# The loads of the modulation weights, issued from POOL's queue instead of SP's

## The chip, the cores and the metric

The kernel runs on one core of a Trainium2 chip. The metric is device time in microseconds (us), the median of several runs. A profiled execution gives the trace; its span runs from the first instruction to the last.

The core has five engines with an instruction queue each: PE (matmul; its weight loads are listed as PEld), DVE, ACT, POOL (all three elementwise) and SP, which here only issues transfers. Each queue is worked through in order.

## The reference, cut to what matters

A decoder trunk of two layers on one sequence of 512 tokens, 1024 wide. Every sub-layer sees its input normalised, scaled and shifted by a modulation that comes from one conditioning vector `c`, and its output is multiplied by a gate from the same modulation:

```
cond = silu(c)
for layer in range(2):
    mod = cond @ ada_w[layer] + ada_b[layer]        # ada_w[layer]: 1024 x 6144
    shift_m, scale_m, gate_m, shift_f, scale_f, gate_f = split(mod, 6)
    h = rms_norm(x) * (1 + scale_m) + shift_m
    mixed = mixer(h) @ w_out                        # layer 0: S5 and HGRN2; layer 1: GLA
    x = x + gate_m * mixed
    h = rms_norm(x) * (1 + scale_f) + shift_f
    x = x + gate_f * ((silu(h @ w1) * (h @ w3)) @ w2)
return rms_norm(x)
```

All values are float32. `ada_w` has 12 pieces of 1024 x 1024 floats: six for each layer.

## The kernel before

**Activations and products.** Tokens lie along the free dimension: a tile is 128 features x 512 tokens. A matmul in full precision is made of three: `proj` (L269) splits each weight tile and each activation into a high and a low part and sums high x high, high x low and low x high. For each weight tile `wload` (L253) loads `raw` from SP (`wraw`, L241, three buffers), ACT copies it to `whi` and DVE subtracts to get `wlo` (`wsplit`, L246, three buffers each). So PE lives on splits that ACT and DVE make some tiles ahead.

**Modulation.** Two pieces, shift and scale of layer 0's mixer, are computed at once at the start (`ada_first`, L390) from loads of their own (L383). The other ten are made step by step beside the products. `ada_run` (L192) is a generator: for each entry of `later` it runs 8n steps on DVE, n = 4 for two pieces together, n = 2 for one. A step multiplies 128 x 512 weights by a column of `cond` and adds them to `acc` (L204, the first of an entry is L202); at the end four small matmuls fold `acc` over the partitions (L210). The steps keep their program order on DVE.

**Their loads.** `ada_loads` (L179) feeds the steps. One tile `wr` (tag "ar", two buffers) is 128 x 2 x 512 floats, 512 KB, and serves two steps. It is filled by n transfers: four of 32 partitions (128 KB) or two of 64 partitions (256 KB). In program order the tile for the next pair of steps is asked for one pair ahead. There are 64 tiles of four transfers and 16 of two, 288 in all. The first tiles also wait for `bn` and `cn`, S5 inputs that use the same two buffers (L649).

**Where the steps fall.** `ada_steps` (L226) is called at the end of each `wload` and runs up to `pace[0]` steps, up to a number of pieces. In layer 0's mixer the pace is 3 and later 8, in the FFN 2 for each weight tile. `ada_need` (L233) runs what is left when a piece is used: the gate of the mixer's output (L431), the norm ahead of the FFN (L366), the FFN's gate. In `later` the order is: layer 0's pieces 2 and 4, then 3, then 5, then three pairs for layer 1, which are made during layer 0's FFN.

**What sets the order.** The tile framework plans the order of each engine's instructions with a timing model (`schedule_with_timeline_sim`, L1252), and it places every wait. A transfer waits for its buffer to be free, on the engine that issues it, and what is queued behind it waits as well.

**POOL's own work.** In layer 0's mixer POOL makes the S5 matrices (`cmul` in `s5_mats`, L698: tiles `B0a`, `W0a` and so on), parts of the S5 rotation (`rz0c`, `rz0d` and their like, L788 to L800, between DVE's scans of L792), and gates (`hg`, `ys`). Later it has only sums for the norms (`na_f`, `na_m`, L335) and the gates of layer 1 (`gr`). It issues no transfer.

Of the kernel before, what the change touches and what calls it, by code (L numbers as in the profile page):

```python
# [19 lines left out]
T = 512  # L20
# [21 lines left out]
def trunk(  # L42
# [8 lines left out]
    nc = tc.nc  # L51
    x = x[0]
    out = out[0]
# [125 lines left out]
    def ada_loads():  # L179
        for l, pieces in later:  # L180
            n = 2 * len(pieces)
            r = P // n
            src = ada_w[l].rearrange("(k z r) n -> k r z n", z=2, r=r)
            for k in range(4 * n):
                wr = wp.tile([P, 2, T], F32, tag="ar", name=f"ar{l}{pieces[0]}{k}", bufs=2)
                for g in range(n):
                    c0 = pieces[g // 2] * D + g % 2 * T
                    nc.sync.dma_start(out=wr[g * r : g * r + r], in_=src[k, :, :, c0 : c0 + T])
                for j in range(2):
                    yield wr[:, j, :]  # L190

    def ada_run():  # L192
        loads = ada_loads()
        nxt = [next(loads) for _ in range(2)]
        for l, pieces in later:
            n = 2 * len(pieces)
            acc = ap.tile([P, T], F32, tag="acc", name=f"acc{l}{pieces[0]}", bufs=1)
            for k in range(8 * n):
                nxt.append(next(loads, None))
                w, c_ = nxt.pop(0), conds[n][:, k : k + 1]  # L200
                if k == 0:
                    ins = V.tensor_scalar(out=acc, in0=w, scalar1=c_, scalar2=None, op0=ALU.mult)  # L202
                else:
                    ins = V.scalar_tensor_tensor(out=acc, in0=w, scalar=c_, in1=acc, op0=ALU.mult, op1=ALU.add)  # L204
                tc.keep_in_program_order(ins)
                if k + 1 < 8 * n:
                    yield
            fp = ps_b(f"fold{l}{pieces[0]}")[:, 0 : 4 * n]
            for m in range(4):
                ins = PE.matmul(fp[:, m::4], lhsT=acc[:, m * P : (m + 1) * P], rhs=ind[n], start=True, stop=True)  # L210
                if m == 0:
                    tc.keep_in_program_order(ins)
            for j, i in enumerate(pieces):
                c0 = i * 8
                ttv(V, mod[:, l, c0 : c0 + 8], fp[:, j * 8 : j * 8 + 8], cols1[:, l * 48 + c0 : l * 48 + c0 + 8], ALU.add)
                if i in (1, 4):
                    g0 = 96 + (i // 4) * 16 + l * 8
                    stt(gsc[:, l * 2 + i // 4, :], mod[:, l, c0 : c0 + 8], 1.0, cols1[:, g0 : g0 + 8], ALU.add, ALU.mult)
                done.add((l, i))
            yield  # L220
# [921 lines left out]
    for hd in range(4):  # L1142
# [18 lines left out]
        c0 = 1024 + hd * 256  # L1161
        vt = tok_tiles(win[:, c0 : c0 + 2 * P], f"gv{hd}", keep, tag)
        c0 = 2048 + hd * 256
# [92 lines left out]
```

## Time and profile before

| | |
|---|---|
| median of 3 runs | 1357.15 us |
| lowest and highest | 1355.7, 1358.05 us |
| profiled execution | 1364.62 us |
| its span | 1362.8 us |
| its mean granted clock of PE | 0.967 of full |

The profiled execution lies 7.47 us above the median and its span 1.82 us below its own time. Times in the views count from the start of the span.

### The profile page before, as it was taken

What the parts mean: (1) busy time and instruction counts of PE and PEld (TensorE: products, weight loads), DVE (VectorE), ACT (ScalarE), POOL (GpSimd) and SP (SyncE); (2) the same over time, 40 slices, a digit from 0 to 9 for tenths busy, and PEclk for the clock granted to TensorE, in tenths of its full rate; (3) what the DMA queues carried; (4) which work ended last, traced back from release to release, by engine and by line L of the source; (5) the groups of instructions that cost most, each with busy time, mean ns of one, the idle gap of its engine ahead of it and who ended that gap; (6) DMA issues with size and microseconds to landing.
All of it is one profiled execution on the core that took longest, in us unless ns stands there. A gap on an engine that the chain in (4) does not pass through costs nothing.

```text
span 1362.8 us, 18262 instructions
## 1 busy us (share of the span) xinstructions
PE 1286.2 (94%) x6949; PEld 1103.4 (81%) x6949; DVE 797.2 (58%) x1511; ACT 487.5 (36%) x851; POOL 151.0 (11%) x148
## 2 busy tenths in 40 slices
PE   6598899799899999999999999999899999999997
PEld 3377887778888888888889999998788888888886
DVE  4979796887865566665445446557653333333344
ACT  5253556423532322222334434432442322232232
POOL 1764451120100000000000000000100000000000
PEclk9779998889899999999999999999999999999999
DMA  8624540534067768987333232213223323433222
GB/s 293 163 63 129 150 140 16 126 94 132 18 142 188 202 174 213 214 219 198 106 106 94 65 92 63 74 49 97 62 82 104 93 74 103 117 93 93 79 86 83
DMA packets 222824, 159.69 MB, mean 117 GB/s; under 512 B 16752, under 2 KB 195248, under 8 KB 222736
## 3 DMA queue, kind: packets, MB, share of 16 engines
q1 hardware_dynamic: 221696, 157.48, 42.2%
q10 hardware_dynamic: 1040, 1.05, 0.3%
q8 instruction: 54, 0.88, 0.3%
q14 instruction: 34, 0.28, 0.1%
HBM read 156.40 MB, written 2.10 MB: 116 GB/s over the span
## 4 chain that ended last, share of the span: by engine, by line
PE 78%; DVE 12%; DMA 4%; ACT 2%; issue 2%; POOL 1%; SPq 0%; DVEq 0%; ACTq 0%
PE f L275 18%; PE f L276 18%; PE f L277 18%; DMA ar<-in_ada_w_dram 3%; PE op L276 2%; PE op L275 2%; PE op L277 2%; PE lv_g L465 2%; DVE acc L204 2%; PE gr L300 1%; PE gr L301 1%; PE gr L299 1%; PE gv L301 1%; PE gv L300 1%; PE gv L299 1%
## 5 line engine op out<-in xcount | busy, mean ns | idle before, releaser
L276 PE MATMUL f<-hlo_f,whi_f 128*128 128x512 f32 (+1 forms) x736 | 281.5, 383 | 0.2 <-DVE hlo_f L116 0.2
L275 PE MATMUL f<-hhi_f,whi_f 128*128 128x512 f32 (+1 forms) x736 | 280.9, 384 | 0.5 <-ACT hhi_f L86 0.5
L277 PE MATMUL f<-hhi_f,wlo_f 128*128 128x512 f32 (+1 forms) x736 | 280.8, 382 | 0.0
L86 ACT ACTIVATE whi_f<-raw_f 128x1024 fp32r<-128x1024 f32 x88 | 93.3, 1061 | 307.0 <-PE f L276 169.3
L107 DVE TENSOR_TENSOR wlo_f<-raw_f,whi_f 128x1024 fp32r<-128x1024 f32 x88 | 107.7, 1224 | 115.1 <-ACT whi_f L86 114.8
L276 PEld LDWEIGHTS f<-hlo_f,whi_f 128*128 128x128 f32 x736 | 140.1, 190 | 27.0 <-DVE hlo_f L116 0.8
L275 PEld LDWEIGHTS f<-hhi_f,whi_f 128*128 128x128 f32 x736 | 139.8, 191 | 27.0 <-ACT hhi_f L86 1.0
L277 PEld LDWEIGHTS f<-hhi_f,wlo_f 128*128 128x128 f32 x736 | 140.1, 191 | 26.5
L204 DVE SCALAR_TENSOR_TENSOR acc<-ar,cond,acc 128x512 f32<-128x512 f32 x154 | 120.1, 780 | 41.6 <-DMA ar<-in_ada_w_dram 40.0
L277 PE MATMUL f<-hi_g,wlo_c 128*128 128x512 f32 x312 | 121.7, 390 | 0.0
L276 PE MATMUL f<-lo_g,whi_c 128*128 128x512 f32 x312 | 121.6, 390 | 0.0
L275 PE MATMUL f<-hi_g,whi_c 128*128 128x512 f32 x312 | 121.2, 390 | 0.0
L86 ACT ACTIVATE whi_c<-raw_c 128x768 fp32r<-128x768 f32 (+1 forms) x56 | 44.9, 801 | 161.8 <-PE f L276 114.1
L107 DVE TENSOR_TENSOR g<-g,f 128x512 f32<-128x512 f32 x44 | 30.3, 688 | 109.3 <-PE f L277 109.3
L107 DVE TENSOR_TENSOR wlo_c<-raw_c,whi_c 128x768 fp32r<-128x768 f32 (+1 forms) x56 | 50.3, 898 | 57.6 <-ACT whi_c L86 57.5
L276 PEld LDWEIGHTS f<-lo_g,whi_c 128*128 128x128 f32 x312 | 58.6, 188 | 12.1
L275 PEld LDWEIGHTS f<-hi_g,whi_c 128*128 128x128 f32 x312 | 58.6, 188 | 12.1
L277 PEld LDWEIGHTS f<-hi_g,wlo_c 128*128 128x128 f32 x312 | 58.6, 188 | 12.1
L116 DVE SCALAR_TENSOR_TENSOR x<-f,mod,x 128x512 f32<-128x512 f32 (+1 forms) x36 | 24.8, 689 | 39.4 <-PE f L277 39.2
L107 POOL TENSOR_TENSOR na_m<-na_m,nsq_m 128x256 f32<-128x256 f32 x7 | 5.7, 818 | 365.3 <-DMA raw_c<-in_ffn_w_dram 337.9
L300 PE MATMUL gv<-wlo_gv,hhi_m 128*128 128x256 f32 x128 | 36.7, 287 | 0.0
L301 PE MATMUL gv<-whi_gv,hlo_m 128*128 128x256 f32 x128 | 36.6, 286 | 0.0
(667 smaller groups left out, 2677.9 us busy)
## 6 DMA issues: line engine op xcount, KB each, us to landing
raw_f<-in_ffn_w_dram SPq DMA_DIRECT2D x88, 512.0 KB, 3.8
ar<-in_ada_w_dram SPq DMA_DIRECT2D x256, 128.0 KB, 3.7
ar<-in_ada_w_dram SPq DMA_DIRECT2D x64, 256.0 KB, 5.3
raw_c<-in_ffn_w_dram SPq DMA_DIRECT2D x32, 384.0 KB, 3.5
raw_c<-in_ffn_w_dram SPq DMA_DIRECT2D x24, 320.0 KB, 3.2
raw_gv<-in_od_w_in_dram SPq DMA_DIRECT2D x8, 512.0 KB, 4.4
raw_gr<-in_od_w_in_dram SPq DMA_DIRECT2D x8, 512.0 KB, 4.0
raw_o<-in_ev_w_out_dram SPq DMA_DIRECT2D x8, 384.0 KB, 3.4
```

The lines of the kernel that those rows point to most:

```text
L86: return A.activation(out=o, in_=i, func=f, **kw)
L107: e.tensor_tensor(out=o, in0=a, in1=b, op=op)
L116: V.scalar_tensor_tensor(out=o, in0=a, scalar=s, in1=b, op0=op0, op1=op1)
L204: ins = V.scalar_tensor_tensor(out=acc, in0=w, scalar=c_, in1=acc, op0=ALU.mult, op1=ALU.add)
L275: PE.matmul(ps, lhsT=hi, rhs=ah[:, ts], start=(i == 0), stop=False)
L276: PE.matmul(ps, lhsT=hi, rhs=al[:, ts], start=False, stop=False)
L277: ins = PE.matmul(ps, lhsT=lo, rhs=ah[:, ts], start=False, stop=(i == n - 1))
L299: PE.matmul(o, lhsT=ah[:, s], rhs=hi, start=(k == 0), stop=False)
L300: PE.matmul(o, lhsT=ah[:, s], rhs=lo, start=False, stop=False)
L301: PE.matmul(o, lhsT=al[:, s], rhs=hi, start=False, stop=(k == KT - 1))
L465: PE.matmul(ps[0:nk, w, :].rearrange("p (n b) -> p n b", b=b), lhsT=K[:, w * P : w * P + nk], rhs=qv[:, w * nb : (w + 1) * nb, b:], start= ...
```

## The change

Only the queue on which the loads of `ada_loads` are issued is another: POOL's (`nc.gpsimd`) for SP's (`nc.sync`). The tiles, their buffers, the 288 transfers, their sizes and the steps that use them stay. The loads of L383 stay on SP.

```
@@ -185,7 +185,7 @@
                 wr = wp.tile([P, 2, T], F32, tag="ar", name=f"ar{l}{pieces[0]}{k}", bufs=2)
                 for g in range(n):
                     c0 = pieces[g // 2] * D + g % 2 * T
-                    nc.sync.dma_start(out=wr[g * r : g * r + r], in_=src[k, :, :, c0 : c0 + T])
+                    nc.gpsimd.dma_start(out=wr[g * r : g * r + r], in_=src[k, :, :, c0 : c0 + T])
                 for j in range(2):
                     yield wr[:, j, :]
```

## Rows read from the trace of the kernel before

**Rows 1.** The page's totals: busy us, share of the span, instructions.

```profile
PE 1286.2 (94%) x6949; PEld 1103.4 (81%) x6949; DVE 797.2 (58%) x1511; ACT 487.5 (36%) x851; POOL 151.0 (11%) x148
```

**Rows 2.** The chain that ended last, share by engine and by line.

```profile
PE 78%; DVE 12%; DMA 4%; ACT 2%; issue 2%; POOL 1%; SPq 0%; DVEq 0%; ACTq 0%
PE f L275 18%; PE f L276 18%; PE f L277 18%; DMA ar<-in_ada_w_dram 3%; PE op L276 2%; PE op L275 2%; PE op L277 2%; PE lv_g L465 2%; DVE acc L204 2%; PE gr L300 1%; PE gr L301 1%; PE gr L299 1%; PE gv L301 1%; PE gv L300 1%; PE gv L299 1%
```

**Rows 3.** Busy time by stretch: length, engines, clock, DMA share, GB/s.

```profile
95.00:153.00 58.00, 50.48 (x306) 45.32 (x306) 48.64 (x95) 28.14 (x62) 24.06 (x16) 0.94 0.52 145
153.00:195.00 42.00, 37.15 (x301) 36.37 (x299) 40.42 (x70) 18.76 (x43) 17.98 (x15) 0.96 0.52 139
250.00:285.00 35.00, 27.48 (x139) 24.78 (x139) 29.23 (x76) 17.96 (x47) 5.32 (x4) 0.80 0.57 135
...
495.00:565.00 70.00, 70.00 (x314) 58.09 (x313) 42.62 (x59) 14.89 (x18) 0.00 (x0) 1.00 0.85 203
```

**Rows 4.** Line L188 over the whole span: ns min/median/max; who waited for it.

```profile
L188 SPq DMA_DIRECT2D ar<-in_ada_w_dram x288: 311/421/1852, 63.4 to 657.2; - x144
  DVE acc L204: 40.0, 25
```

**Rows 5.** Waits by engine (us, times, longest), 60 to 375, then 375 to 700.

```profile
DVE acc L204 <- DMA ar<-in_ada_w_dram: 10.6, 5, 4.2
SPq L188 <- DVE acc L204: 26.5, 14, 5.9
...
DVE acc L204 <- DMA ar<-in_ada_w_dram: 29.4, 20, 3.1
SPq L188 <- DVE acc L204: 70.1, 52, 3.8
```

**Rows 6.** The page's DMA queues: packets, MB, share of 16 engines.

```profile
q1 hardware_dynamic: 221696, 157.48, 42.2%
q10 hardware_dynamic: 1040, 1.05, 0.3%
```

**Rows 7.** POOL in order of time: start, us, instruction, idle time before it.

```profile
115.31 7.25 POOL L107 TENSOR_TENSOR rz0c<-rz0c,rz0d 128x512 f32<-128x512 f32 x1 [24.73 <-DVE rz0d L107]
126.28 1.26 POOL L107 TENSOR_TENSOR rz0d<-rz0d,cos 128x512 f32<-128x512 f32 x1
142.40 0.74 POOL L107 TENSOR_TENSOR B2b<-B2b 128x256 f32<-128x256 f32 x1
157.57 3.27 POOL L107 TENSOR_TENSOR rz1c<-rz1c,rz1d 128x512 f32<-128x512 f32 x1 [12.54 <-DVE rz1d L107]
193.88 5.41 POOL L107 TENSOR_TENSOR rz2c<-rz2c,rz2d 128x512 f32<-128x512 f32 x1 [7.48 <-DVE rz2d L107]
```

**Rows 8.** Line L188 from 95 to 153, 153 to 195, 250 to 285 us.

```profile
L188 SPq DMA_DIRECT2D ar<-in_ada_w_dram x36: 311/425/672, 101.6 to 148.8; - x36
  DVE acc L204: 5.2, 2
...
L188 SPq DMA_DIRECT2D ar<-in_ada_w_dram x24: 311/424/710, 153.1 to 191.4; - x24
...
L188 SPq DMA_DIRECT2D ar<-in_ada_w_dram x16: 595/597/608, 254.5 to 283.4; - x16
```

**Rows 9.** DVE in order of time in the FFN: steps on `acc`.

```profile
523.44 1.54 DVE L204 SCALAR_TENSOR_TENSOR acc<-ar,cond,acc 128x512 f32<-128x512 f32 x2 [1.00 <-DMA ar<-in_ada_w_dram]
...
531.67 1.54 DVE L204 SCALAR_TENSOR_TENSOR acc<-ar,cond,acc 128x512 f32<-128x512 f32 x2 [0.93 <-DMA ar<-in_ada_w_dram]
...
563.17 1.54 DVE L204 SCALAR_TENSOR_TENSOR acc<-ar,cond,acc 128x512 f32<-128x512 f32 x2 [2.81 <-DMA ar<-in_ada_w_dram]
```

**Rows 10.** SP's queue in order of time in the FFN.

```profile
525.01 1.72 SPq L188 DMA_DIRECT2D ar<-in_ada_w_dram  x4
526.83 0.39 SPq L243 DMA_DIRECT2D raw_c<-in_ffn_w_dram  x1
```

**Rows 11.** Line L188 from 495 to 565 us, and its transfers' time to landing.

```profile
L188 SPq DMA_DIRECT2D ar<-in_ada_w_dram x61: 311/418/1208, 496.3 to 564.7; - x61
...
DMA to landing us min/median/max: 2.5/5.3/6.9
```

More of the change, by code (lines that the diff above doesn't have):

```diff
@@ L187, in ada_loads @@
                     c0 = pieces[g // 2] * D + g % 2 * T
-                    nc.sync.dma_start(out=wr[g * r : g * r + r], in_=src[k, :, :, c0 : c0 + T])
+                    nc.gpsimd.dma_start(out=wr[g * r : g * r + r], in_=src[k, :, :, c0 : c0 + T])
                 for j in range(2):
```

## Prediction

> **What bounds the kernel now.** I read the page's totals first, then the chain that ended last, then busy time by stretch, then who waits for the loads of L188, and at last POOL's own row in time. The totals [rows 1] show PE busy for 94% of the span and POOL for 11%: on average POOL has room. The chain [rows 2] gives PE 78%, DVE 12%, DMA 4% and SP's queue 0%: the engine that loses work under this change is not on the path, the loads themselves are, with about 3%.
>
> The stretches have different limits [rows 3]. From 95 to 195 us (layer 0's mixer) DVE is busy 48.64 of 58 us and then 40.42 of 42; PE is not full, so here lateness on DVE is lateness of the kernel. POOL is far from idle there: 24.06 + 17.98 = 42.0 of 100 us. From 495 to 565 us (layer 0's FFN) PE is busy 70.00 of 70 us and POOL does nothing: here a late load costs only what outlasts the split weights already made for PE.
>
> DVE waited for `ar` tiles for 40.0 us in 25 places, 10.6 of them before 375 us and 29.4 after [rows 4, 5]. The 29.4 us lie beside a full PE and cost nothing today; so what could be won is near 10 us.
>
> **The change, part by part.** *SP loses* 288 issues of 0.421 us [rows 4], 121 us in all, and its waits for a free `ar` buffer, 26.5 us before 375 us and 70.1 after [rows 5]; weight loads queued behind those waits go out earlier. SP is not on the chain, and the loads that it then issues sooner still wait for their own three buffers. I count a gain of 2 us, out of the 10.6 us at most.
>
> *POOL gains* 288 issues. The trace has no transfer issued by POOL: all of it runs on hardware queues [rows 6]. So the price c of one issue is bounded by rows: below by SP's 0.42 us, above by a full POOL instruction on 128x512, 1.26 us undisturbed [rows 4, 7]. POOL's half-size instruction takes 0.74 us [rows 7]. A transfer here is 128 KB in rows of 2 KB (512 floats), 64 rows, and making up 64 places to read and write seems nearer to POOL's ordinary work than to SP's; I take 1.0 us, the middle of 0.74 and 1.26, and keep 0.42 and 1.26 as ends.
>
> The Trainium skill ("DMA: Bandwidth & Descriptors", Specifications) gives about 1 us to the first byte on the GpSimd path against 0.6 on the other; read as an estimate of c it would give the same sum as mine.
>
> *Mixer, 95 to 195 us.* SP issues 36 + 24 = 60 loads there [rows 8]. On POOL they take 60 x 1.0 = 60 us; with the 42.0 us of its own work that is 102 us in 100. POOL also stands still in order, waiting for DVE: 12.54 us ahead of `rz1c`, 7.48 ahead of `rz2c` [rows 7]. A load behind such a wait is late; an issue that waits for `acc` to free a buffer holds back what is behind it on POOL: the S5 products (`rz1c`, on which DVE's scans wait, and `B2a`, `W2a`, from which PE's S5 matrices are made). On DVE the steps on `acc` keep program order, so behind a step that waits for its tile stand the splits `wlo`, and PE waits for those. Lower bound of the cost: 0, if the planner fits the issues into POOL's waits. Upper: the 2 us over plus both waits, 22 us. I take 10, near the middle, since nothing says which way the planner goes.
>
> *250 to 285 us.* 16 issues of 256 KB, 0.597 us each on SP [rows 8]; at 1.0 us 0.4 x 16 = 6.4 us longer, from 0 to 6.4 on the path as DVE is 29.23 of 35 busy [rows 3]. I take 3.
>
> *FFN, with PE full.* One tile (four issues) feeds two steps. PE's matmuls there take 70.00 / 314 = 0.223 us; a half-column weight tile of the second product (six blocks, three matmuls each) keeps PE 18 x 0.223 = 4.01 us, and one `ar` tile is consumed for each. The steps on DVE came at 523.44, 527.67, 531.67 and so on to 563.17: 9 gaps, 4.41 us each [rows 9]. One buffer's circle is: steps end at 524.98, SP issues from 525.01 to 526.73, the steps on that tile begin at 531.67, 4.94 us after the last issue, and take 1.54 [rows 9, 10]. Two buffers share it, so a tile takes (4c + 4.94 + 1.54) / 2 = 2c + 3.24 us: 4.1 at 0.42, 5.24 at 1.0, 5.76 at 1.26. If the spread issues land as the fastest do now, 2.5 us after issue [rows 11], it is 2c + 2.02: 4.02 at 1.0. Between 4.02 and 5.24 I take the middle, 4.63. About 15 tiles lie there (61 issues [rows 11]): 15 x (4.63 - 4.01) = 9.3 us behind PE, against a cover of two split weight tiles in three buffers, 8.0 us; 1.3 us come through, 10.5 at 5.24. I take 4. In the first products a weight tile is 24 matmuls, 5.35 us, so 5.24 fits and costs nothing; without that fit each 0.1 us over costs 3.3 us, for some 33 tiles (48 + 6 less 15 and a few).
>
> *Sum:* -2 + 10 + 3 + 4 = +15 us on a span of 1362.8. The profiled execution took 1364.62, 7.5 above the median of the runs, 1357.15; I carry the difference over: 1372. With c = 0.42: about 0 less the 2, 1355. With c = 1.26: mixer 60 x 1.26 + 42 - 100 = 18 (the waits filled), 250 to 285 us 5, FFN 15 x (5.76 - 4.01) - 8 = 18 and 33 x 0.41 = 13.5; less 2, +53, that is 1410.
>
> **The rivals.** *POOL's issues are stretched* (slower still). For it: POOL's 128x512 instruction took 7.25 us at `rz0c` and 5.41 at `rz2c` against 1.26 elsewhere, while DVE ran its own two-input instructions; DVE does so in the FFN too, as the steps on `acc` show [rows 7, 9]. Against it: an issue need not read tiles as those products do. It decides from c = 5.35 / 4 = 1.34 us, where four issues alone outlast the longer weight tile. At 1.6: tile 6.44 us, FFN 15 x 2.43 - 8 = 28 and 33 x 1.09 = 36, mixer 60 x 1.6 + 42 - 100 = 38, last burst 8; +108, 1465.
>
> Beside it, the Trainium skill ("SBUF — State Buffer", SBUF: two separate sides) warns that DVE's fast copies keep POOL from writing its transfer lists, where transfers issued from SP are immune. The rows show such stretching only for POOL's arithmetic; no transfer of POOL is in this trace.
>
> *Hidden* (no change). If c is 0.74 or less, POOL's load in the mixer is 60 x 0.74 + 42 = 86 us in 100, and the FFN tile takes at most 4.72 us: 15 x 0.71 - 8 = 2.7. With the planner's order favourable the sum lies between -2 and +5: 1355 to 1362. The chain's 0% for SP speaks for it [rows 2], the thin cover in the FFN against it.
>
> The Trainium skill ("DMA: Bandwidth & Descriptors", Issuing engines are not separate DMA queues) says the same of such moves: all queues share the same engines, only time at the issuing engine is saved.
>
> *Freed order* (faster). One mechanism: on SP a load of `ar` stands behind weight loads that wait for a buffer, and on POOL, if its own work leaves gaps there, it goes out the moment `acc` frees one. DVE's 10.6 us before 375 us [rows 5] shrink, and DVE is what limits that stretch: up to 8 us, 1349. It decides if a group of four issues takes no longer than SP's 1.72 us plus the wait saved; against it, the longest waits fall where the issues run back to back and the transfer itself is awaited [rows 8], and POOL has waits of its own.
>
> **How the numbers follow.** A measurement of this kernel tells about 0.2% (2.7 us) from no change. Forecast, c between 0.85 and 1.34, +6 to +55: 0.48, likeliest 1372, own range 1363 to 1412. Stretched: 0.12. Hidden: 0.22, of which 0.15 within 0.2% and 0.07 slower. Freed order: 0.18. So faster 0.18, same 0.15, slower 0.48 + 0.12 + 0.07 = 0.67. The range 1351 to 1415 leaves out the stretched case and about 0.07 of the faster one.
>
> **What the profile after would show.** Queue issues of L188 on POOL with their length (c, the main unknown: under 0.75 the forecast falls to hidden, over 1.34 to stretched); a queue of POOL's own beside those of [rows 6], with the 42 MB of these loads (256 x 128 KB and 32 x 256 KB) taken from q1; POOL's instructions `rz0c` to `rz2c` later, with waits for L204 ahead of them; DVE waits for `ar` above 10.6 us before 375 us; gaps between pairs of steps in the FFN above 4.41 us and the first idle time of PE between 495 and 610 us. The clock was 0.94 to 0.96 of full in the mixer [rows 3]; a PE idle for longer there may see it fall, for which I price nothing. Wrong would make it: a planner that moves POOL's products so that the issues never meet them, or one that puts them behind a wait of 20 us.

## Result, and the profile after

The changed kernel takes 1378.23 us (median of 4 runs, 1377.13 to 1381.51) against 1357.6 (4 runs, 1355.7 to 1362.3) for the kernel before beside it: a ratio of 1.0151, 95% interval 1.0119 to 1.0182. It is slower, within the range and 6 us above the predicted 1372. The profiled execution took 1377.59 us with a span of 1375.8, 13.0 us more than the 1362.8 before.

First the page's totals after, then the chain that ended last, by engine and by line.

```profile
PE 1288.1 (94%) x6949; PEld 1104.7 (80%) x6949; DVE 802.7 (58%) x1511; ACT 487.5 (35%) x851; POOL 293.0 (21%) x436
...
PE 80%; DVE 11%; ACT 4%; issue 2%; DMA 1%; POOL 1%; SPq 0%; DVEq 0%; POOLq 0%; ACTq 0%
PE f L275 18%; PE f L276 18%; PE f L277 17%; ACT yf L86 2%; PE op L275 2%; PE op L276 2%; PE op L277 2%; PE lv_g L465 2%; PE lv_h L465 1%; PE gr L300 1%; PE gr L301 1%; PE gr L299 1%; PE gv L301 1%; PE gv L300 1%; PE gv L299 1%
```

Against [rows 1] POOL is what has changed: 288 instructions and 142 us more, and still 79% idle. Against [rows 2] the loads of `ar` have left the list (3% before; all DMA is 1% now), ACT's copies `yf` of S5's output have come on it with 2%, and POOL stays at 1%. The totals hide the loss; the issues themselves are next. The view of L188 over the whole span:

```profile
L188 POOL DMA_DIRECT2D ar<-in_ada_w_dram x288: 533/536/726, 66.4 to 669.4; - x144
...
  DVE acc L204: 44.3, 26
...
DMA to landing us min/median/max: 2.5/3.6/7.1
```

So c is 0.536 us, and no issue of all 288 took over 0.726. A queue of POOL's own took the bytes from q1, as the page's DMA queues show (beside [rows 6]):

```profile
q1 hardware_dynamic: 196608, 115.52, 29.7%
q0 software_dynamic: 14848, 41.96, 11.8%
```

Busy time by stretch, columns as in [rows 3], with 195 to 250 us added:

```profile
95.00:153.00 58.00, 51.42 (x330) 46.26 (x330) 51.08 (x95) 19.07 (x39) 34.05 (x44) 0.97 0.54 143
153.00:195.00 42.00, 34.54 (x230) 32.95 (x228) 35.57 (x51) 16.61 (x36) 27.75 (x37) 0.84 0.33 97
195.00:250.00 55.00, 51.23 (x345) 46.22 (x345) 38.63 (x82) 29.24 (x68) 23.83 (x27) 0.94 0.32 87
250.00:285.00 35.00, 19.87 (x109) 18.52 (x108) 26.39 (x78) 14.02 (x43) 7.36 (x8) 0.66 0.23 58
495.00:565.00 70.00, 70.00 (x314) 58.10 (x313) 42.05 (x59) 15.36 (x20) 29.90 (x57) 1.00 0.78 190
```

In the mixer POOL is busy 34.05 + 27.75 = 61.8 of 100 us, not over-full. DVE, the limit there before, now idles: 35.57 busy of 42 from 153 to 195 us against 40.42. And from 250 to 285 us PE has a hole: 19.87 busy against 27.48, at a granted clock of 0.66 against 0.80. The kernel is late by then, so the window holds other work than before; in the 35 us ahead of the product `glu` in each trace PE is busy 20.05 us after (258.1 to 293.1) and 26.20 before (236.6 to 271.6). In the FFN PE is full, as before. The waits, from 60 to 375 us and then from 375 to 700 (beside [rows 5]):

```profile
POOL ar L188 <- DVE acc L204: 77.1, 18, 16.4
DVE acc L204 <- DMA ar<-in_ada_w_dram: 8.0, 6, 3.0
...
POOL ar L188 <- DVE acc L204: 171.6, 48, 24.0
DVE acc L204 <- DMA ar<-in_ada_w_dram: 36.3, 20, 4.3
```

POOL now stands 77.1 us ahead of issues that wait for `acc` to free a buffer. What stands behind them shows POOL in order of time, with the rows that answer to [rows 7]:

```profile
100.74 2.14 POOL L188 DMA_DIRECT2D ar<-in_ada_w_dram  x4 [16.44 <-DVE acc L204]
109.95 2.11 POOL L188 DMA_DIRECT2D ar<-in_ada_w_dram  x4 [7.08 <-DVE acc L204]
112.08 1.95 POOL L107 TENSOR_TENSOR B1a<-s5b,s5L 128x256 f32<-128x256 f32 x2
113.99 8.02 POOL L107 TENSOR_TENSOR B1b<-s5b,s5L 128x256 f32<-128x256 f32 x2
...
124.30 1.25 POOL L107 TENSOR_TENSOR rz0c<-rz0c,rz0d 128x512 f32<-128x512 f32 x1
...
172.26 1.47 POOL L107 TENSOR_TENSOR rz1c<-rz1c,rz1d 128x512 f32<-128x512 f32 x1
...
224.76 4.88 POOL L107 TENSOR_TENSOR rz2c<-rz2c,rz2d 128x512 f32<-128x512 f32 x1 [3.56 <-DVE rz2d L107]
```

`B1a` begins 28.7 us later (it began at 83.33), behind two tiles' issues; `rz0c` 9.0 us later, `rz1c` 14.7, `rz2c` 30.9. Of `rz0c`'s 9.0 us only 3.0 reach DVE, for `rz0c` itself took 7.25 us before and 1.25 after. The scans of DVE that wait for it, before and then after:

```profile
122.59 1.90 DVE L792 TENSOR_TENSOR_SCAN rz0d<-s5s,rz0c 128x128 f32<-128x128 f32 x4 [1.20 <-POOL rz0c L107]
...
125.58 1.73 DVE L792 TENSOR_TENSOR_SCAN rz0d<-s5s,rz0c 128x128 f32<-128x128 f32 x2 [4.05 <-POOL rz0c L107]
```

The scans on `rz1d` begin 17.7 us later (182.94 against 165.27), those on `rz2d` 31.7 (233.28 against 201.56). Further milestones, by first start in the two traces:

| | before | after | later by |
|---|---|---|---|
| `rz3c` on POOL | 241.5 | 263.4 | 21.9 |
| `glu` on PE | 271.6 | 293.1 | 21.5 |
| FFN's first product `f` on PE | 366.6 | 380.6 | 14.0 |
| end of the span | 1362.8 | 1375.8 | 13.0 |

The loss is made by 263 us: from `rz3c` to `glu` both traces take about 30 us, hole or not. Some 8 us come back before the FFN, and from there to the end before takes 996.2 us and after 995.2. The profiled execution of before was one of that kernel's longer ones (1364.62 us against a median of 1357.6), that of after lies 0.64 us under its median: the two traces differ by 13.0 us, the medians by 20.6.

### The profile page after: what moved, and what is told of

Read it like the earlier page. It is cut to its first block, busy times and chain, and to the rows that moved or that the text cites. A ratio compares the mean times of both kernels' runs of the same rounds, so it can differ in the third digit from the quotient of the medians.

```text
span 1375.8 us, 18333 instructions
## 1 busy us (share of the span) xinstructions
PE 1288.1 (94%) x6949; PEld 1104.7 (80%) x6949; DVE 802.7 (58%) x1511; ACT 487.5 (35%) x851; POOL 293.0 (21%) x436
## 3 DMA queue, kind: packets, MB, share of 16 engines
q1 hardware_dynamic: 196608, 115.52, 29.7%
## 4 chain that ended last, share of the span: by engine, by line
PE 80%; DVE 11%; ACT 4%; issue 2%; DMA 1%; POOL 1%; SPq 0%; DVEq 0%; POOLq 0%; ACTq 0%
PE f L275 18%; PE f L276 18%; PE f L277 17%; ACT yf L86 2%; PE op L275 2%; PE op L276 2%; PE op L277 2%; PE lv_g L465 2%; PE lv_h L465 1%; PE gr L300 1%; PE gr L301 1%; PE gr L299 1%; PE gv L301 1%; PE gv L300 1%; PE gv L299 1%
## 5 line engine op out<-in xcount | busy, mean ns | idle before, releaser
L188 POOL DMA_DIRECT2D ar<-in_ada_w_dram x288 | 155.1, 545 | 262.1 <-DVE acc L204 248.7
L107 DVE TENSOR_TENSOR wlo_f<-raw_f,whi_f 128x1024 fp32r<-128x1024 f32 x88 | 107.7, 1224 | 109.4 <-ACT whi_f L86 109.1
L107 DVE TENSOR_TENSOR g<-g,f 128x512 f32<-128x512 f32 x44 | 30.2, 687 | 107.1 <-PE f L277 107.1
L107 DVE TENSOR_TENSOR wlo_c<-raw_c,whi_c 128x768 fp32r<-128x768 f32 (+1 forms) x56 | 50.2, 897 | 56.4 <-ACT whi_c L86 56.4
```

The costliest lines, as they stand in the source:

```text
L107: e.tensor_tensor(out=o, in0=a, in1=b, op=op)
L188: nc.gpsimd.dma_start(out=wr[g * r : g * r + r], in_=src[k, :, :, c0 : c0 + T])
```

## Experiments

Each ratio is to runs of the kernel before beside it. "The order held" means that the kernel is planned twice: a first plan gives each engine's order of instructions, and the second build adds order edges that hold PE, ACT and DVE to it (POOL and SP stay with the planner). The added code moves the named lines down by up to 23 (L188 is L191 in e3, L107 is L113 in e5 and e10).

**Where: e1 and e2.** Only layer 1's 192 loads, made in layer 0's FFN, go to POOL (e1), or only layer 0's 96, most of them in the mixer (e2).

```
e1: (nc.gpsimd if l else nc.sync).dma_start(out=wr[...], ...)
e2: (nc.sync if l else nc.gpsimd).dma_start(out=wr[...], ...)
```

> Only the loads of layer 1's pieces (192 of 288, all issued during layer 0's FFN) go on POOL's queue; the 96 for layer 0's pieces stay on SP. Theory A (the loss is made in layer 0's mixer, where POOL's S5 products stand in its queue behind issues that wait for acc): no change, 1355 to 1360 us. Theory C (each issue on POOL costs a little everywhere, or the FFN's loads run late behind a full PE): two thirds of the loss, near 1371 us.

> The other part alone: only the 96 loads of layer 0's pieces go on POOL, layer 1's stay on SP. Theory A: all of the loss, 1374 to 1380 us. Theory C: a third of it, near 1364 us.

e1: 1362.07 us, 1.0025 (0.9999 to 1.0052). e2: 1382.57, 1.0178 (1.0154 to 1.0203). Both lie 2 to 3 us above the ranges of theory A. All of the loss that is clear of noise is in layer 0's 96 loads; e1's interval leaves up to 0.5% to layer 1's. The same stretch of the FFN as above, in e1:

```profile
495.00:565.00 70.00, 70.00 (x315) 58.05 (x314) 40.78 (x57) 15.68 (x18) 30.45 (x58) 1.00 0.87 200
```

POOL works 30.45 us there and PE stays full.

**Queue or plan: e3, e4 and e8.** The planner also put the other engines in another order. e3 has all loads on POOL and holds PE, ACT and DVE to the order of the plan of before; e4 has all loads on SP and holds them to the plan of the changed kernel; e8 is e4 with DVE alone held.

```
+    plan = orders(build(lambda nc: nc.sync))        # e4, e8: nc.gpsimd
+    nc = build(lambda nc: nc.gpsimd, plan)          # e4, e8: nc.sync
...
+    for names in plan.values():                     # one list per held engine
+        last = None
+        for n in names:
+            if n in here:
+                if last is not None:
+                    tc.add_manual_dep(here[n], last, order, ...)   # order only, no wait
+                last = n
```

> All 288 loads on POOL, but the order of the instructions of PE, ACT and DVE is held to that of the kernel before; only POOL's and SP's own order is the planner's. Theory A (POOL's queue in order is the cause): still slow, 1370 us or more. Theory B (the planner, reckoning with its own price of a POOL issue, put PE's, ACT's and DVE's work in a worse order): back to 1355 to 1361 us.

> The reverse: all 288 loads on SP, but PE, ACT and DVE held to the order of the changed kernel. Theory A: 1355 to 1361 us, since no product stands behind a load. Theory B: 1374 to 1380 us. In between, both have a share, and the two runs together give it.

> All loads on SP, DVE's order alone held to the plan of the changed kernel, PE and ACT left to the planner (e4 held all three: 1368.5 against 1359.8 for before). If DVE's order carries the plan's loss: 1366 to 1370. If it is PE's or ACT's order: 1357 to 1362.

e3: 1371.9 us, 1.011 (1.0074 to 1.0145). e4: 1368.52, 1.0078 (1.0047 to 1.0109). e8: 1366.69, 1.006 (1.0042 to 1.0077). Neither theory holds alone: the queue costs some 1.1% in the old order, and the new order some 0.8% without any load on POOL. DVE's order, with PE and ACT left to the planner, gives most of the latter; why that order is the slower one no run shows. Busy time by stretch in e4, where POOL issues nothing:

```profile
195.00:250.00 55.00, 45.70 (x303) 40.92 (x303) 34.49 (x80) 37.09 (x99) 16.66 (x13) 0.87 0.20 52
250.00:285.00 35.00, 19.27 (x105) 17.85 (x105) 29.25 (x71) 14.09 (x28) 4.68 (x3) 0.70 0.37 90
```

PE's hole from 250 to 285 us, with the lower clock, is there (19.27 busy at 0.70; after has 19.87 at 0.66). It belongs to the order, not to the queue (ahead of `glu`, from 247.8 to 282.8 us, PE is busy 19.16 of 35).

**POOL's time and POOL's waits, without a load on POOL: e6, e9, e10.** All loads on SP, the order of before held, and extra work on POOL for each of layer 0's 96 loads. In e6 that is two fills of an unused tile, which wait for nothing; in e9 the first fill of a tile waits, as an issue would, for the step on `acc` that frees the tile's buffer; e10 has that wait with one fill of 128x1 for a tile.

```
+                    if l == 0:
+                        for z in range(2):                    # e10: one of 128x1, where g == 0
+                            new = G.memset(fill, 0.0).ins     # 128 x 208
+                            if g + z == 0:                    # e9, e10; e6: an order edge behind the load
+                                tc.add_manual_dep(new, last_step_on_acc, sync, ...)
```

> All loads on SP, orders of PE, ACT and DVE held to the plan of before; behind each of the 96 mixer loads POOL gets two small fills of an unused tile (128 x 208 floats), which wait for nothing: about 0.5 us of POOL's time for each load, as an issue takes on POOL, without its wait. The fills are extra work and feed nothing. Theory A (blocking by waits): within 0.3% of before, 1356 to 1363 where before is at 1359. Rival T (POOL's time): the loss of e3 comes back, 1368 to 1373.

> As e6 (all loads on SP, orders of PE, ACT and DVE held to the plan of before, 192 small fills on POOL), but now the first fill of each tile waits for the step on acc that frees the tile's buffer, as an issue on POOL does; the fills are extra work and feed nothing. So POOL has the waits and nearly the time of e3's issues, in e3's places of its queue, while the loads themselves go out on SP when they did before. Theory P (the queue's loss is made on POOL: its products stand behind waits for acc): the time of e3, 1368 to 1373, with B1a near 103 us and rz0c near 122. Rival U (the loss is made by the loads, which go out later behind POOL's products and behind its waits for DVE, as e5's 22.2 us of waits for ar suggest): the time of e6, 1360 to 1364.

> As e9, but one fill of 128x1 for each tile in place of eight of 128x208: the waits alone, next to no time of POOL. Theory P: 1364 to 1372, close to e9. Rival U: as before, 1357 to 1361. If wait and time are needed together (an issue that begins late and then keeps POOL for 4 x 0.54 us): e9 near 1370 and this one at 1360 to 1364.

e6: 1362.1 us, 1.0026 (1.0009 to 1.0044), as theory A expected. e10: 1362.31, 1.0024 (1.0006 to 1.0043). e9: 1364.81, 1.0051 (1.0033 to 1.0069). The fills of e6 took 192 x 0.273 = 52.5 us, as much as 96 issues would. So POOL's time costs about 0.25%, the waits as much, and both together the sum, within these intervals. The order of before held with nothing added was not run; in the traces of e6 and e10 PE, DVE, ACT and SP's issues follow the order of before throughout, and 7 and 5 of POOL's 148 other instructions stand in other places, so little else can be in the 0.25%. e9 is half of e3; it lies between theory P, which wanted 1368 to 1373, and rival U with 1360 to 1364, and e10 just above U's 1357 to 1361. POOL in order of time in e10:

```profile
100.62 0.10 POOL L201 MEMSET fill<- 128x1 f32 x1 [18.25 <-DVE acc L220]
100.67 1.21 POOL L113 TENSOR_TENSOR B1a<-s5b,s5L 128x256 f32<-128x256 f32 x2
...
115.29 3.50 POOL L113 TENSOR_TENSOR rz0c<-rz0c,rz0d 128x512 f32<-128x512 f32 x1 [1.29 <-DVE rz0d L113]
```

`B1a` is 17 us late and `rz0c` begins where it did before (115.31), DVE's scans on it too (122.78 us, 122.59 before): group 1's products had slack. That products behind a wait are dear only where `rz0c` or its like is among them is suggested by this, not shown.

**Products first: e5 and e7, which did not do what they were to.** An order edge puts the ninth load on POOL behind the products of group 1, the 41st behind those of group 2; e5 on top of e3, e7 with every order free.

```
+    for q, n in ((1, 8), (2, 40)):
+        tc.add_manual_dep(ar_loads[n], last_product[q], order, ...)
```

> As e3 (all loads on POOL, orders of PE, ACT and DVE held to the plan of before: 1371.9 us, against 1359.8 for before beside it), but on POOL the ninth load has to stand behind all twelve products of the S5 matrices of group 1, and the 41st behind those of group 2; number and time of the issues are the same. Theory A (the loss of the queue is made by products that stand behind issues waiting for acc): B1a starts near 84 us instead of 103, as before (83.3), and part of e3's 12 us comes back, for group 2's first products still have 20 loads ahead of them: 1362 to 1367. Rival T (what costs is POOL's time for the issues, 96 x 0.54 = 52 us in the mixer, or the later issue of the loads): 1370 to 1374.

> As the changed kernel (all loads on POOL, every engine's order left to the planner), with the two orders of e5 added: the ninth load behind the products of group 1, the 41st behind those of group 2. Theory A with the plan as a second, separate loss (e4: +0.8%): the queue's part shrinks, the plan's stays: 1366 to 1373 against 1378 to 1380 for the changed kernel. If the plan's loss is itself made by the late products in the planner's model, both come back: 1360 to 1364. Rival T: 1376 to 1382.

e5: 1378.2 us, 1.0141 (1.012 to 1.0163), above all ranges. e7: 1380.99, 1.0162 (1.0142 to 1.0182), in the range of rival T. The edge held one of a tile's four loads; the planner left the other three ahead. POOL in order of time in e5, and under it DVE's step that uses that tile:

```profile
101.16 1.63 POOL L194 DMA_DIRECT2D ar<-in_ada_w_dram  x3 [15.56 <-DVE acc L210]
102.80 1.85 POOL L113 TENSOR_TENSOR B1a<-s5b,s5L 128x256 f32<-128x256 f32 x2
...
115.85 1.30 POOL L113 TENSOR_TENSOR rz0c<-rz0c,rz0d 128x512 f32<-128x512 f32 x1 [5.13 <-DVE rz0d L113]
117.11 0.73 POOL L113 TENSOR_TENSOR W1b<-W1b 128x256 f32<-128x256 f32 x1
117.78 2.67 POOL L194 DMA_DIRECT2D ar<-in_ada_w_dram  x5
```

```profile
120.76 0.75 DVE L210 SCALAR_TENSOR_TENSOR acc<-ar,cond,acc 128x512 f32<-128x512 f32 x1 [4.98 <-DMA ar<-in_ada_w_dram]
```

`B1a` gained nothing, the fourth load waited until 117.78, and DVE stood 4.98 us for it. On DVE the waits for `ar` from 60 to 330 us went from e3's 14.3 us to 22.2. In e7 those waits were 7.4 us. The runs don't answer the question they were made for, and e7 doesn't speak for rival T; e5 shows the other side of the queue, a load held behind products.

**The loads bound too: e11 and e12.** e11 is e9, and each tile's first load on SP also waits for that first fill. In e12 POOL's order is e3's own, place for place, with two fills for every issue of layer 0, and each load on SP waits for the first of its own fills. (In e9 and e11 the planner had split a tile's fills and put products between them.)

```
+                    tc.add_manual_dep(ld.ins, first_fill, sync, ...)   # e11: where g == 0; e12: each load
+    plan["Pool"] = e3's order on POOL, each of its issues replaced by its two fills   # e12
```

> As e9 (loads on SP, orders of PE, ACT and DVE held to the plan of before, fills on POOL whose first one waits for the step that frees the tile), and each tile's first load on SP now also waits for that first fill: it goes out no sooner than its place on POOL's queue comes up, behind POOL's products. Both halves of the coupling are there, and no transfer is issued by POOL. If the rest of e3's loss (1.1%, against 0.5% in e9) is the loads going out later behind POOL's own work: 1368 to 1374, with waits for ar on DVE above e9's 13.5 us. If it belongs to something of POOL's own issue (its length, its transfers): 1362 to 1366, as e9. SP's weight loads stand behind the added wait too, which can only add to the first case.

> As e11, but POOL's order is now e3's own, place for place: each of the 96 issues of the mixer is replaced by two fills of 128x208 (about 0.5 us), in groups as e3's issues stand, the first of a tile waits for the step that frees the tile, and each load goes out on SP no sooner than its own fills' place on POOL. In e9 and e11 the planner had split these groups and put products between them. Theory V (the rest of e3's loss, 1.1% against 0.45% in e11, is the order on POOL: whole groups of issues ahead of products that DVE's scans wait for): 1370 to 1375, with the first sums of group 1 after 114 us and the 13th load near 124. Rival W (it belongs to the issue or the transfers of POOL's own kind): 1363 to 1367, as e11.

e11: 1365.73 us, 1.0045 (1.003 to 1.0059), no more than e9 and in the range named for a rest that belongs to POOL's own issues. e12: 1368.49, 1.0067 (1.0044 to 1.0089), between theory V and rival W. Busy time by stretch in e12:

```profile
153.00:195.00 42.00, 36.01 (x275) 34.92 (x273) 38.85 (x64) 17.19 (x40) 33.20 (x63) 0.92 0.45 126
...
250.00:285.00 35.00, 27.12 (x148) 24.73 (x147) 30.16 (x65) 15.71 (x43) 12.32 (x28) 0.80 0.50 119
```

With the old order PE has its 27 us from 250 to 285, at the clock of before. DVE is busy 38.85 us from 153 to 195 us, 40.42 before [rows 3], but e6 and e10 have 38.93 and 38.43 there too; DVE's scans on `rz3d` begin 5.1 us later than before (251.20 against 246.13).

**The account.** Queue with the old order: 1.1%, of which 0.67% is shown with no transfer issued by POOL: its time, its waits, and the places of both in one queue. The other 0.4% is open, and the intervals of e3 and e12 overlap (1.0074 to 1.0089). One difference stands in the traces' mixers: e3's issues ended 2.16 us after 112.06, and the sum `B1b` that then began took 6.90 us where e12's took 1.21, so that `rz0c` began at 122.47 in e3 and 116.17 in e12. Only 1.1 us of it reached DVE's scans (123.75 and 122.66). At `rz3d` the scans of e3 are 5.0 us behind e12's (256.23 and 251.20), but PE's first product `f` of the FFN begins at nearly the same time in both (e3's line first):

```profile
L278 PE MATMUL f<-hhi_f,whi_f x736: 277/389/582, 371.4 to 1301.5; 128*128 128x512 f32 x168, 128*128 128x256 f32 x16
...
L299 PE MATMUL f<-hhi_f,whi_f x736: 278/389/582, 371.0 to 1299.2; 128*128 128x512 f32 x168, 128*128 128x256 f32 x16
```

From there to the end e3 takes 998.2 us and e12 996.4. So the rest need not be the mixer's: e3 has layer 1's 192 loads on POOL as well, e12 has not, and e1's interval leaves room for them (up to 0.5%), though the traces of e1 (996.4 us) and of after (995.2) show no cost there. e12 with layer 1's loads on POOL was not run. New order alone: 0.8%. The sum, 1.9%, is not clearly more than the 1.5% and 1.8% measured of the whole (after, e2).

## Why the prediction was right, point by point

**Direction and place** held: slower, made in layer 0's mixer. **The mechanism** held in part: issues that wait for `acc` stand ahead of the S5 products in POOL's single queue, and by e3 that is some 1.1%; the changed order of the other engines, 0.8%, was not priced. The rows gave the first part beforehand: DVE nearly full there, POOL with waits of its own [rows 3, 7]. The second path, loads that come late and hold up DVE's steps, was not seen: DVE's waits for `ar` before 375 us fell to 8.0 us, where the sign asked for more than 10.6.

**The price c** was mis-sized: 1.0 us taken, 0.536 measured, near SP's 0.42 and not near POOL's arithmetic [rows 4, 7]. The argument that making up 64 rows is like POOL's ordinary work was wrong. By the prediction's own sign, a c under 0.75, its forecast would have fallen to *Hidden*, 1355 to 1362, and by its own sum POOL has 60 x 0.536 + 42.0 = 74.2 us of work in 100. That 1372 came near is in good part luck: the mixer's 10 was picked between 0 and 22, and about as much came from an order of the other engines that stood in no term.

**Mixer, +10.** "102 us in 100" did not come: POOL was busy 61.8 of 100 us, and its time by itself costs about 0.25%, 3.5 us (e6). Waits cost as much again (e10). What the planner does was left as "nothing says which way the planner goes" and priced, for POOL's queue alone, between 0 and 22; that it would also reorder PE, ACT and DVE stood in no term, and it costs 0.8%, some 10 us (e4), as much as the whole term. In the traces all 13 us of the span are made ahead of the FFN; by e3 and e4 some two fifths of the loss is not queueing but the changed order.

**250 to 285 us, +3.** Wrong step. The 256 KB issues there cost what they did on SP (median 0.589 us in this stretch, 0.597 before [rows 8]). PE was busy 7.6 us less in the window, at a clock of 0.66, for the order's sake (e4 has the hole with no load on POOL). For the fallen clock nothing had been priced, and no cost of the hole shows: from `rz3c` to `glu` after takes 29.7 us, before 30.1.

**FFN, +4.** None is seen. The circle's own formula gives that with the measured c: 2 x 0.536 + 3.24 = 4.31 us for a tile, 15 x (4.31 - 4.01) = 4.5 us behind PE, under the cover of 8.0. DVE's waits for `ar` after 375 us grew from 29.4 to 36.3 us, beside a full PE, and from the first `f` to the end after takes no longer than before (995.2 and 996.2 us). e1's 1.0025, with 1 inside its interval, can't tell 4 us from none. Line L188 and two of DVE's steps in that stretch, beside [rows 9, 11]:

```profile
L188 POOL DMA_DIRECT2D ar<-in_ada_w_dram x57: 533/536/542, 497.7 to 564.7; - x57
```

```profile
545.54 1.54 DVE L204 SCALAR_TENSOR_TENSOR acc<-ar,cond,acc 128x512 f32<-128x512 f32 x2 [2.75 <-DMA ar<-in_ada_w_dram]
...
554.22 1.54 DVE L204 SCALAR_TENSOR_TENSOR acc<-ar,cond,acc 128x512 f32<-128x512 f32 x2 [2.06 <-DMA ar<-in_ada_w_dram]
```

**SP's relief, -2.** Not seen by itself. DVE's waits for `ar` up to 375 us fell from 10.6 to 8.0 us, and no time came of it.

**Rivals.** *Stretched*: refuted, the longest issue took 0.726 us where it needed 1.34. *Hidden*: its condition, c up to 0.74, was met, and nothing was hidden. It was set on the wrong quantity: POOL's sum of work, where the order of two chains in one queue decided. The Trainium skill ("DMA: Bandwidth & Descriptors", Issuing engines are not separate DMA queues) says that such a move saves no more than time at the issuing engine; the runs agree: SP was rid of 288 issues and no time came of it, though from issue to landing the median fell a little, to 3.6 us from 3.8 over the whole span. e9 and e4 show what the new issuing engine and the plan can lose. *Freed order*: refuted, the mixer loses, and e1 gains nothing in the FFN.

**The sum**, +15, met +13.0 in the spans and +20.6 in the medians. The difference of 7.7 us is the profiled executions': that of before stood 7.0 us above its median, that of after 0.6 below. The prediction took the first as a constant; the second has none of it. By the medians, the better measure of the two kernels, the loss is 20.6 us and the sum was some 6 short of it, as 1372 was.

## What to carry to other kernels

Before a wait is moved to an engine that computes, list what that engine feeds and compare it with what the wait hangs on: two chains that both run through DVE can lose when one in-order queue holds both, however idle the engine is on average. Where a planner orders the work, a moved instruction reorders the engines it never touches; hold their order and run again, and queue and plan can be priced apart. A condition on an engine's sum of work says little; price the first instruction behind each wait by who waits for it.

## What the runs showed of the hardware

- An issue on POOL took 0.536 us (median) for 128 KB in 64 rows of 2 KB; SP's took 0.42. For 256 KB POOL's took 0.592 (16 issues from 277.8 to 308.6 us), SP's 0.597: POOL's length hardly grew with the transfer, SP's did.
- POOL's issues were not stretched beside DVE as POOL's arithmetic is: at most 0.726 us, and 0.536 in the median of the 178 that ran beside a TENSOR_TENSOR or SCALAR_TENSOR_TENSOR of DVE, while two products `B1b` from 113.99 us on took 8.02 us together. The Trainium skill ("SBUF — State Buffer", SBUF: two separate sides) warns of DVE's copies keeping POOL from its transfer lists; no issue here shows it, but only three ran beside a copy on DVE (0.536 to 0.552 us).
- PE's granted clock: after, from 250 to 255 us PE was busy for only 0.71 us, and in the next stretch the clock was 0.50, the lower of the two levels, 1.2 GHz against 2.4. The windows of it:

```profile
250.00:255.00 5.00, 0.71 (x5) 0.42 (x4) 2.70 (x10) 4.82 (x14) 0.00 (x0) 0.84 0.00 0
255.00:260.00 5.00, 3.04 (x12) 2.74 (x13) 0.86 (x8) 4.97 (x22) 0.00 (x0) 0.50 0.00 0
275.00:280.00 5.00, 2.64 (x10) 2.35 (x11) 5.00 (x19) 0.00 (x0) 1.21 (x2) 0.50 0.40 107
```

The 0.66 of the longer stretch is a mean of the two levels, as is the 0.80 of before.
